# Moving all nine adaLN modulations of a two-layer trunk onto TensorE, 512 columns at a time in four column groups

## The chip, the cores and the metric

The kernel runs on one core of one Trainium2 chip. The metric is the device time of one execution in microseconds (us); lower is better. Three timed runs of the kernel before are shown, and one profiled execution.

## What is computed

The reference is one step of a diffusion trunk of two layers. 384 tokens of width 1024 pass through it: 128 context tokens and 256 latent tokens. Each layer is a SwiGLU, a token mixer of four parallel branches, and a second SwiGLU, all with residuals. Ahead of each of the three, the residual is normalised, scaled and shifted by vectors that depend on a conditioning vector; a third vector gates the result. These nine vectors of 1024 are the modulations of the layer:

```python
mod = jnp.einsum('bd,de->be', jax.nn.silu(cond), lp['w_ada']) + lp['b_ada']
mod = mod.reshape(cond.shape[0], N_MOD, 1, D_MODEL)
h = rms_norm(x, lp['norm_g'][0]) * (1.0 + mod[:, 1]) + mod[:, 0]
x = x + 0.5 * mod[:, 2] * swiglu(h, lp['ffn_w_gate'][0], lp['ffn_w_up'][0], lp['ffn_w_down'][0])
h = rms_norm(x, lp['norm_g'][1]) * (1.0 + mod[:, 4]) + mod[:, 3]
mix, state = token_mix(h, lp, l, cache)
x = x + mod[:, 5] * mix
h = rms_norm(x, lp['norm_g'][2]) * (1.0 + mod[:, 7]) + mod[:, 6]
x = x + 0.5 * mod[:, 8] * swiglu(h, lp['ffn_w_gate'][1], lp['ffn_w_up'][1], lp['ffn_w_down'][1])
```

There are two conditionings, one for the context tokens and one for the latent tokens, so each modulation is a product of two vectors of 1024 with a matrix of 1024 by 1024. `w_ada` has 9216 columns a layer. Modulations 0 and 1 of layer 0 are needed before the first SwiGLU can begin.

## The kernel before

The residual lies in the core's memory with its features on the 128 partitions and the 384 tokens as columns. Products of weights and residual are done in three matmuls, `mm3` (lines 184 to 188): weights and residual are each split into a rounded part and a rest, and hi by hi, hi by lo and lo by hi are added up. `split_unit` (lines 165 to 174) makes the two parts of a piece of weights: ScalarE casts to `whi` (line 169), VectorE or GpSimd subtracts to get `wlo` (line 173). There are three buffers of each.

A SwiGLU (`ffn_body`, lines 443 to 499) is a loop over 11 pieces of the hidden width, each with one load of gate weights and one of up weights of 1 MB and 96 matmuls (tiles `pg` and `pu`), and then a loop of the down product in two halves (tile `pd`), 528 matmuls. That is 1056 + 528 = 1584 matmuls of 384 columns for each of the four SwiGLUs. In this text FFN 0.0 and 0.1 are the two of layer 0, FFN 1.0 and 1.1 those of layer 1, and the mixers lie between the two of a layer.

The modulations are computed in quarters of 256 columns, in two ways:

- `ada` (lines 258 to 292) loads a quarter of 1024 by 256, 1 MB, as a tile `araw`. For the context conditioning VectorE multiplies and adds eight slices (lines 268 and 271). For the latent one ScalarE multiplies (lines 269 and 274) and GpSimd adds (line 275). VectorE transposes in blocks and reduces (lines 278 and 279), and at the end of a call four matmuls with a selection matrix put the sums on the partitions (line 285, tile `xa`).
- `ada_rows` (lines 238 to 256) does a quarter on TensorE: eight f32 matmuls with a stationary operand of two columns, one for each conditioning, and 256 moving columns (line 246, tile `arow`), a copy and two transposes.

`start` (lines 372 to 398) computes modulations 0 and 1 of layer 0: three quarters with `ada`, five with `ada_rows`, in the order of the string `ORDER`. All other quarters run beside the SwiGLUs. `hook(n)` takes n of them after each of the 11 pieces (line 469) and one after each part of the down loop (line 492), at a priority lowered by 100. FFN 0.0 has 28 quarters, FFN 0.1 has 20, FFN 1.0 has 16, and FFN 1.1 has none.

The order of the instructions on each engine is set when the kernel is built: a scheduler puts them in the order of a simulated timeline and of their priorities. All loads named here are issued by SP, in one queue, in that order, and a load that waits for its buffer holds up the loads behind it.

Of the kernel before, what the change touches and what calls it, by code (L numbers as in the profile page):

```python
# [17 lines left out]
D = 1024  # L18
# [16 lines left out]
K_ID, K_SEL, K_ONE = 0, 128, 640  # L35
# [8 lines left out]
ORDER = "nsrsrsrrr"  # L44
RING, NT1, NT2 = 256 * 310, 6, 4
# [4 lines left out]
def host_constants():  # L50
# [12 lines left out]
    for r in range(4):  # L63
        c[:, K_SEL + 128 * r:K_SEL + 128 * (r + 1)] = i[None, :] == (32 * r + i[:, None] % 32)
# [15 lines left out]
def pack_vectors(x):  # L80
    """The small vectors of both layers as columns of 128."""
# [14 lines left out]
def lockstep(*tasks):  # L96
    """Issue several tasks a stage of each at a time."""
    tasks = list(tasks)
    while tasks:
        tasks = [t for t in tasks if next(t, t) is not t]  # L100


class Ring:
    """Tiles at consecutive offsets of one window of memory, each over the oldest ones."""
# [13 lines left out]
class Trunk:  # L118
# [75 lines left out]
    def hidden(self, w, name="mm"):  # L194
        """A product with the normed residual; the first ones are scaled by 1 / rms and shifted behind the product."""
# [17 lines left out]
    def setup(self):  # L213
# [10 lines left out]
        nc.scalar.activation(out=self.cond, in_=vec[:, 0:16], func=AF.Silu)  # L224
        xrs = []
# [12 lines left out]
    def ada_rows(self, l, quarters):  # L238
        """Quarters of the nine modulations on the tensor engine, for both conditionings."""
        nc = self.nc  # L240
        cond = self.cond.rearrange("p (s k) -> p k s", s=2)
        for mod, j in quarters:
            raw = self.wcols(self.I["w_ada"][l], mod * D + 256 * j)
            ps = self.pm.tile([2, 256], F32, tag="mm", name="arow")
            for kk in range(KD):
                nc.tensor.matmul(ps, cond[:, kk], raw[:, kk], start=(kk == 0), stop=(kk == KD - 1))
            row = self.ring.tmp([2, 256], "mrow")
            nc.scalar.copy(row, ps)
            tp = self.mxps([128, 2, 2])
            for q in range(2):  # L250
                nc.tensor.transpose(tp[:, q], row[:, 128 * q:128 * q + 128], self.k(K_ID)[0:2, 0:2])
            c = slice(8 * mod + 2 * j, 8 * mod + 2 * j + 2)
            nc.vector.tensor_tensor(self.mods[l][:, :, c].rearrange("p s k -> p k s"), tp,
                                    self.prm[l][:, R_B:R_B + 72][:, c].unsqueeze(2).to_broadcast([128, 2, 2]),
                                    op=ALU.add)
            yield

    def ada(self, l, mod, n=4):
        """The same beside the tensor engine, n quarters from a modulation on, one at a time."""
        nc = self.nc  # L260
        ap = self.ap
        xa = ap.tile([128, 2, 8 * n], F32, tag="xa", name="xa", bufs=1)
        for j in range(n):
            raw = ap.tile([128, KD, 256], F32, tag="araw", name="araw", bufs=2)
            c0 = mod * D + 256 * j
            nc.sync.dma_start(raw, self.I["w_ada"][l, :, c0:c0 + 256].rearrange("(k p) n -> p k n", p=128))
            acc = [ap.tile([128, 256], F32, tag="acc", name="acc", bufs=6) for _ in range(2)]
            nc.vector.tensor_scalar_mul(acc[0], raw[:, 0], self.cond[:, 0:1])
            nc.scalar.mul(acc[1], raw[:, 0], self.cond[:, 8:9])
            for kk in range(1, KD):  # L270
                nc.vector.scalar_tensor_tensor(  # L271
                    acc[0], raw[:, kk], self.cond[:, kk:kk + 1], acc[0], op0=ALU.mult, op1=ALU.add)
                t = ap.tile([128, 256], F32, tag="acc", name="acct", bufs=6)
                nc.scalar.mul(t, raw[:, kk], self.cond[:, 8 + kk:9 + kk])  # L274
                self.last_add = nc.gpsimd.tensor_tensor(acc[1], acc[1], t, op=ALU.add)  # L275
            for s in range(2):
                tr = ap.tile([128, 256], F32, tag="acc", name="accr", bufs=6)
                nc.vector.transpose(tr, acc[s])  # L278
                nc.vector.tensor_reduce(
                    xa[:, s, 8 * j:8 * j + 8], tr.rearrange("p (a b) -> p a b", b=32), axis=AX, op=ALU.add  # L280
                )
            yield
        ps = self.mxps([128, 2, 2 * n])
        for r in range(4):
            nc.tensor.matmul(
                ps, self.k(K_SEL + 128 * r), xa.rearrange("p s (k r) -> p s k r", r=4)[:, :, :, r],
                start=(r == 0), stop=(r == 3),
            )
        c = slice(8 * mod, 8 * mod + 2 * n)
        nc.vector.tensor_tensor(self.mods[l][:, :, c], ps,  # L290
                                self.prm[l][:, R_B:R_B + 72][:, c].unsqueeze(1).to_broadcast([128, 2, 2 * n]), op=ALU.add)
        yield
# [79 lines left out]
    def start(self):  # L372
# [22 lines left out]
        with self.after(self.last_add):  # L395
            for k in range(KD):
                self.norm_scale(k)
# [1087 lines left out]
```

## Time and profile before

| | us |
|---|---|
| runs, median of 3 | 2246.99 |
| lowest, highest of the runs | 2241.5, 2248.05 |
| span of the profiled execution | 2244.0 |
| TensorE busy (matmuls) | 2076.3 |
| VectorE busy | 1724.6 |
| ScalarE busy | 1039.3 |
| GpSimd busy | 942.2 |

The span runs from the first to the last instruction of the profiled execution; that execution's own time as a run is not given apart, so sums are made against the span. Busy time is the union of an engine's instructions. Matmuls overlap in the records, so a mean duration is longer than the distance from one matmul to the next; where the price of a matmul is wanted, count the matmuls in a full stretch. An f32 matmul that is not in the rounded form stands as two instructions in the trace. Tile names are those of the program without buffer numbers.

### The profile page before, as it was taken

What the parts mean: (1) busy time and instruction counts of PE and PEld (TensorE: products, weight loads), DVE (VectorE), ACT (ScalarE), POOL (GpSimd) and SP (SyncE); (2) the same over time, 40 slices, a digit from 0 to 9 for tenths busy, and PEclk for the clock granted to TensorE, in tenths of its full rate; (3) what the DMA queues carried; (4) which work ended last, traced back from release to release, by engine and by line L of the source; (5) the groups of instructions that cost most, each with busy time, mean ns of one, the idle gap of its engine ahead of it and who ended that gap; (6) DMA issues with size and microseconds to landing.
All of it is one profiled execution on the core that took longest, in us unless ns stands there. A gap on an engine that the chain in (4) does not pass through costs nothing. (4 is left out here: it accounts for less than half of the span.)

```text
span 2244.0 us, 33102 instructions
## 1 busy us (share of the span) xinstructions
PE 2076.3 (93%) x12150; PEld 1992.7 (89%) x12150; DVE 1724.6 (77%) x3198; ACT 1039.3 (46%) x1978; POOL 942.2 (42%) x855
## 2 busy tenths in 40 slices
PE   6988888999789997998998999999987999999999
PEld 3988788999679997998887999998976899999999
DVE  8999998778995469999899974467999745764433
ACT  5666554634234235765556643354333332463322
POOL 5556666433655237366476520134354531500000
PEclk8999999999889999999999999999998999999999
DMA  9466655444333244566555644344442321444342
GB/s 306 152 217 199 202 198 164 129 136 105 83 81 103 60 164 155 169 210 214 186 193 155 206 135 133 128 146 137 119 95 83 109 76 59 160 134 129 115 139 76
DMA packets 316515, 323.08 MB, mean 144 GB/s; under 512 B 42112, under 2 KB 287296, under 8 KB 315840
## 3 DMA queue, kind: packets, MB, share of 16 engines
q1 hardware_dynamic: 316080, 320.70, 46.1%
q8 instruction: 95, 1.56, 0.3%
q14 instruction: 68, 0.56, 0.1%
q10 hardware_dynamic: 272, 0.26, 0.0%
HBM read 313.25 MB, written 7.69 MB: 143 GB/s over the span
## 5 line engine op out<-in xcount | busy, mean ns | idle before, releaser
L169 ACT CAST whi<-raw 128x1024 fp32r<-128x1024 f32 x422 | 440.2, 1045 | 511.1 <-PE mg L187 133.3
L173 DVE TENSOR_TENSOR wlo<-raw,whi 128x1024 fp32r<-128x1024 f32 x324 | 434.8, 1343 | 226.9 <-ACT whi L169 223.8
L275 POOL TENSOR_TENSOR acc<-acc,acct 128x256 f32<-128x256 f32 x469 | 440.5, 939 | 334.7 <-ACT acct L274 306.4
L173 POOL TENSOR_TENSOR wlo<-raw,whi 128x1024 fp32r<-128x1024 f32 x98 | 244.9, 2505 | 289.9 <-ACT whi L169 244.2
L271 DVE SCALAR_TENSOR_TENSOR acc<-araw,cond,acc 128x256 f32<-128x256 f32 x469 | 323.5, 690 | 6.3
L274 ACT ACTIVATE acct<-araw,cond 128x256 f32<-128x256 f32 x469 | 214.1, 501 | 139.7 <-DVE accr L278 83.4
L188 PE MATMUL pd<-hh,wlo 128*128 128x384 f32 x704 | 240.8, 345 | 20.2 <-DVE wlo L173 20.2
L186 PE MATMUL pd<-hh,whi 128*128 128x384 f32 x704 | 240.5, 342 | 9.0 <-ACT whi L169 4.5
L187 PE MATMUL pd<-hl,whi 128*128 128x384 f32 x704 | 239.9, 341 | 0.0
L188 PE MATMUL pg<-hhi,wlo 128*128 128x384 f32 x544 | 184.8, 340 | 19.2 <-DVE wlo L173 19.0
L188 PE MATMUL pu<-hhi,wlo 128*128 128x384 f32 x544 | 184.7, 340 | 13.4 <-DVE wlo L173 13.1
L186 PE MATMUL pg<-hhi,whi 128*128 128x384 f32 x544 | 182.1, 335 | 0.4 <-ACT whi L169 0.4
L187 PE MATMUL pu<-hlo,whi 128*128 128x384 f32 x544 | 182.2, 335 | 0.0
L186 PE MATMUL pu<-hhi,whi 128*128 128x384 f32 x544 | 182.2, 335 | 0.0
L187 PE MATMUL pg<-hlo,whi 128*128 128x384 f32 x544 | 182.1, 335 | 0.0
L186 PE MATMUL mg<-hhi,whi 128*128 128x384 f32 x512 | 177.7, 347 | 0.0
L187 PE MATMUL mg<-hlo,whi 128*128 128x384 f32 x512 | 175.4, 343 | 0.0
L188 PE MATMUL mg<-hhi,wlo 128*128 128x384 f32 x512 | 174.5, 343 | 0.5 <-DVE wlo L173 0.5
L321 POOL TENSOR_SCALAR xg<-xT,gs 128x128 f32<-128x128 f32 (+1 forms) x96 | 101.9, 1074 | 150.9 <-DVE xT L432 150.8
L188 PEld LDWEIGHTS pd<-hh,wlo 128*128 128x128 f32 x704 | 134.0, 191 | 27.6 <-DVE wlo L173 27.6
L186 PEld LDWEIGHTS pd<-hh,whi 128*128 128x128 f32 x704 | 134.4, 191 | 11.3 <-ACT whi L169 5.4
L187 PEld LDWEIGHTS pd<-hl,whi 128*128 128x128 f32 x704 | 134.5, 191 | 0.1
(410 smaller groups left out, 4961.5 us busy)
## 6 DMA issues: line engine op xcount, KB each, us to landing
araw<-in_w_ada SPq DMA_DIRECT2D x67, 1024.0 KB
raw<-in_w_in SPq DMA_DIRECT2D x62, 1024.0 KB
raw<-in_ffn_w_gate SPq DMA_DIRECT2D x44, 1024.0 KB
raw<-in_ffn_w_up SPq DMA_DIRECT2D x44, 1024.0 KB
raw<-in_ffn_w_down SPq DMA_DIRECT2D x40, 1024.0 KB
raw<-in_w_branch SPq DMA_DIRECT2D x16, 512.0 KB
raw<-in_w_out SPq DMA_DIRECT2D x8, 1024.0 KB
raw<-in_w_ada SPq DMA_DIRECT2D x5, 1024.0 KB
```

Source lines behind the costliest of these rows:

```text
L169: nc.scalar.copy(hi, src)
L173: (eng or nc.vector).tensor_tensor(lo, src, hi.bitcast(F32), op=ALU.subtract)
L186: nc.tensor.matmul(ps, w[0], x[0], start=start, stop=False)
L187: nc.tensor.matmul(ps, w[0], x[1], start=False, stop=False)
L188: nc.tensor.matmul(ps, w[1], x[0], start=False, stop=stop)
L271: nc.vector.scalar_tensor_tensor(acc[0], raw[:, kk], self.cond[:, kk:kk + 1], acc[0], op0=ALU.mult, op1=ALU.add)
L274: nc.scalar.mul(t, raw[:, kk], self.cond[:, 8 + kk:9 + kk])
L275: self.last_add = nc.gpsimd.tensor_tensor(acc[1], acc[1], t, op=ALU.add)
L321: self.nc.gpsimd.tensor_scalar(xg[kk][:, a:e], self.xT[:, kk, a:e], gs[:, s, kk:kk + 1], None, op0=ALU.mult)
```

## The change

`ada_rows` and the old `ada` go. A new `ada` computes halves of 512 columns on TensorE. The 1024 rows of a half come in two loads of 1 MB, each a tile `araw` of four slices of 128 rows. The stationary operand, `cond32`, is the two conditionings padded with zeros to 32 columns. Slice g of a load goes to column group g, the partitions 32g to 32g + 31 of the result. So a half is eight f32 matmuls, and each column group holds the sum over two slices. One copy, four transposes of 128 columns and a reduction over the four groups finish it.

```diff
+        self.cond32 = self.const.tile([128, KD, 32], F32, name="cond32")
+        nc.vector.memset(self.cond32, 0.0)
+        nc.vector.tensor_copy(self.cond32[:, :, 0:2], self.cond.rearrange("p (s k) -> p k s", s=2))
...
+    def ada(self, l, *halves):
+        nc = self.nc
+        for mod, hf in halves:
+            c0 = mod * D + 512 * hf
+            ps = self.mxps([128, 512], "arow")
+            for i in range(2):
+                raw = self.ap.tile([128, 4, 512], F32, tag="araw", name="araw", bufs=self.n_araw)
+                self.last_load = nc.sync.dma_start(raw, self.I["w_ada"][l, 512 * i:512 * i + 512, c0:c0 + 512].rearrange(
+                    "(k p) n -> p k n", p=128))
+                for g in range(4):
+                    nc.tensor.matmul(ps[32 * g:32 * g + 32], self.cond32[:, 4 * i + g], raw[:, g],
+                                     start=(i == 0), stop=(i == 1), tile_position=(0, 32 * g))
+            row = self.ring.tmp([128, 512], "mrow")
             nc.scalar.copy(row, ps)
+            tp = self.mxps([128, 4, 128], "acol")
+            for q in range(4):
+                nc.tensor.transpose(tp[:, q], row[:, 128 * q:128 * q + 128], self.k(K_ID))
+            t = self.small.tile([128, 2, 4], F32, tag="asum", name="asum")
+            nc.vector.tensor_reduce(t, tp.rearrange("p q (g e) -> p e q g", g=4)[:, 0:2], axis=AX, op=ALU.add)
+            c = slice(8 * mod + 4 * hf, 8 * mod + 4 * hf + 4)
+            nc.vector.tensor_tensor(self.mods[l][:, :, c], t,
+                                    self.prm[l][:, R_B:R_B + 72][:, c].unsqueeze(1).to_broadcast([128, 2, 4]), op=ALU.add)
             yield
...
+        for j, _ in enumerate(self.ada(0, (1, 0), (1, 1))):
+            if j == 0:
                 self.rstd()
...
+        for _ in self.ada(0, (0, 0), (0, 1)):
+            pass
         self.early_shift()
...
-            hook(2)
+            hook(1)
         if nxt is None:
             self.nx = None
         else:
             self.norm_begin(*nxt)
-            self.scales(*nxt, self.nx[2])
...
                 hook(1)
+            if nxt is not None and dg == 0:
+                self.scales(*nxt, self.nx[2])
...
+            self.n_araw = 4
             with self.pool("ap") as self.ap:
                 self.start()
+            self.n_araw = 3
...
-                self.ffn(l, 0, self.ada(l, 5, 16) if l else chain(self.ada(l, 2, 12), self.ada(l, 5, 16)), (l, 1))
+                mods = {(0, 0): ((0, 2, 8),), (0, 1): ((0, 8, 9), (1, 0, 3)), (1, 0): ((1, 3, 8),), (1, 1): ((1, 8, 9),)}
+                jobs = [chain(*(self.ada(m, *((k, hf) for k in range(a, e) for hf in range(2)))
+                                for m, a, e in mods[l, i])) for i in range(2)]
+                self.ffn(l, 0, jobs[0], (l, 1))
...
-                self.ffn(l, 1, iter(()) if l else self.ada(1, 0, 20), None if l else (1, 0))
+                self.ffn(l, 1, jobs[1], None if l else (1, 0))
```

The halves are spread over all four SwiGLUs now: 12 in FFN 0.0, 8 in FFN 0.1, 10 in FFN 1.0 and 2 in FFN 1.1, one hook after each piece; four are in the start. The three buffers of `araw` beside the SwiGLUs (four in the start) hold a half and a half. The selection matrices leave the table of constants, and `RING`, the size of the window of temporary memory, goes from 256 * 310 to 256 * 309.

The change moves instructions at three places that matter here. In names such as `pu_1019` the number is a buffer's.

On TensorE, modulation work reached a SwiGLU before only as the four matmuls on `xa` at the end of a call, here in the down product of FFN 0.0:

```order
L186 MATMUL pd_3490<-hh_2805,whi_3807 128x384
L187 MATMUL pd_3490<-hl_2806,whi_3807 128x384
L285 MATMUL mx_3649<-xa_1992,cst_82 128x64 x4
L188 MATMUL pd_3490<-hh_2805,wlo_3808 128x384
L186 MATMUL pd_3491<-hh_2526,whi_3801 128x384
```

Now every half puts eight `arow` matmuls among those of an up product, here in FFN 0.0; the piece shows where the half goes over from its first load to its second:

```order
L185 MATMUL pu_1019<-hhi_339,wlo_991 128x384
L252 MATMUL arow_894<-araw_895,cond32_91 32x512
L183 MATMUL pu_1019<-hhi_339,whi_990 128x384
L184 MATMUL pu_1019<-hlo_340,whi_990 128x384
L252 MATMUL arow_894<-araw_901,cond32_91 32x512
```

The `arow` matmuls stand one by one between matmuls of the up product, and not four together.

On VectorE, a piece of the SwiGLU's gate and up loop was full of products and reductions for the modulations before:

```order
L271 SCALAR_TENSOR_TENSOR acc_946<-araw_944,cond_89,acc_946 128x256
L278 STREAM_TRANSPOSE accr_978<-acc_946 128x256
L278 STREAM_TRANSPOSE accr_981<-acc_947 128x256
L268 TENSOR_SCALAR acc_1132<-araw_1130,cond_89 128x256
L279 TENSOR_REDUCE xa_665<-accr_978 128x8
L464 TENSOR_TENSOR sg_1123<-sg_1123,pu_1098 128x384
L279 TENSOR_REDUCE xa_665<-accr_981 128x8
L271 SCALAR_TENSOR_TENSOR acc_1132<-araw_1130,cond_89,acc_1132 128x256
L173 TENSOR_TENSOR wlo_1280<-raw_1210,whi_1279 128x1024
```

In the same loop now:

```order
L427 TENSOR_TENSOR sg_1044<-sg_1044,pu_1019 128x384
L170 TENSOR_TENSOR wlo_1144<-raw_1074,whi_1143 128x1024
L431 TENSOR_TENSOR hl_1048<-sg_1044,hh_1047 128x384
L170 TENSOR_TENSOR wlo_1148<-raw_1076,whi_1147 128x1024
L260 TENSOR_REDUCE asum_914<-acol_909 128x8
L262 TENSOR_TENSOR mods0_87<-asum_914,vec_83 128x2x4
L427 TENSOR_TENSOR sg_1136<-sg_1136,pu_1111 128x384
```

A half leaves one reduction and one addition on VectorE, between the splits of the weights.

On TensorE at the start, just ahead of the first SwiGLU, quarters of two kinds ended the chain before:

```order
L246 MATMUL arow_386<-raw_384,cond_89 2x256 x8
L246 MATMUL arow_413<-raw_411,cond_89 2x256 x8
L251 MATMUL mx_397<-cst_82,mrow_395 128x2 x2
L251 MATMUL mx_424<-cst_82,mrow_422 128x2 x2
L285 MATMUL mx_428<-xa_182,cst_82 128x12 x4
L186 MATMUL pg_519<-xs_160,whi_511 128x386
```

Now the last two of the four halves do:

```order
L252 MATMUL arow_267<-araw_268,cond32_91 32x512 x4
L252 MATMUL arow_267<-araw_274,cond32_91 32x512 x4
L258 MATMUL acol_282<-cst_82,mrow_280 128x128 x4
L252 MATMUL arow_290<-araw_291,cond32_91 32x512 x4
L252 MATMUL arow_290<-araw_297,cond32_91 32x512 x4
L258 MATMUL acol_305<-cst_82,mrow_303 128x128 x4
L183 MATMUL pg_398<-xs_163,whi_390 128x386
```

Here the four column groups of a load stand together.

## Rows read from the trace of the kernel before

**Rows 1.** The page, busy time (share of the span) and instructions of each engine.
```profile
PE 2076.3 (93%) x12150; PEld 1992.7 (89%) x12150; DVE 1724.6 (77%) x3198; ACT 1039.3 (46%) x1978; POOL 942.2 (42%) x855
```

**Rows 2.** Windows of the start and the four SwiGLUs; columns in the first line.
```profile
core 0: us, PE busy (x) PEld busy (x) DVE busy (x) ACT busy (x) POOL busy (x), PEclk, DMA share, GB/s
0.00:48.60 48.60, 29.24 (x132) 14.20 (x132) 39.62 (x91) 25.91 (x61) 24.57 (x33) 0.88 0.93 300
48.60:382.60 334.00, 297.86 (x1601) 283.12 (x1602) 322.03 (x531) 200.13 (x385) 211.34 (x224) 0.97 0.60 192
...
864.80:1192.40 327.60, 292.31 (x1603) 281.48 (x1602) 310.33 (x508) 194.02 (x373) 192.46 (x201) 0.98 0.59 190
1192.40:1484.50 292.10, 283.25 (x1604) 279.67 (x1603) 195.10 (x314) 137.68 (x235) 80.63 (x86) 0.99 0.47 146
...
1958.20:2239.00 280.80, 280.06 (x1614) 279.35 (x1613) 126.46 (x183) 103.50 (x155) 7.90 (x6) 1.00 0.36 116
```

**Rows 3.** Timeline of TensorE: start us, us, engine, line, operation; two edges.
```profile
48.60 0.69 PE L186 MATMUL pg<-xs,whi 128*128 128x386 f32 x1 [3.34 <-ACT xs L332]
...
2238.67 0.34 PE L188 MATMUL pd<-hh,wlo 128*128 128x384 f32 x1
```

**Rows 4.** Waits of TensorE in FFN 0.0: us in total, times, longest.
```profile
PE pg L188 <- DVE wlo L173: 11.6, 13, 2.1
PE pd L188 <- DVE wlo L173: 11.5, 11, 2.1
```

**Rows 5.** Groups by line and shape: busy us, mean ns of one | idle before.
```profile
L275 POOL TENSOR_TENSOR acc<-acc,acct 128x256 f32<-128x256 f32 x469 | 440.5, 939 | 334.7 <-ACT acct L274 306.4
...
L271 DVE SCALAR_TENSOR_TENSOR acc<-araw,cond,acc 128x256 f32<-128x256 f32 x469 | 323.5, 690 | 6.3
...
L274 ACT ACTIVATE acct<-araw,cond 128x256 f32<-128x256 f32 x469 | 214.1, 501 | 139.7 <-DVE accr L278 83.4 <-POOL acc L275 42.2 <-DVE xa L279 13.3
...
L279 DVE TENSOR_REDUCE xa<-accr 128x8 f32<-128x256 f32 x134 | 50.7, 406 | 0.1
```

**Rows 6.** Windows again, a stretch inside the up product of FFN 1.1.
```profile
2016.00:2072.00 56.00, 56.00 (x325) 56.00 (x324) 24.21 (x28) 19.56 (x28) 0.00 (x0) 1.00 0.45 145
```

**Rows 7.** Timeline of TensorE in the start, and durations (min/median/max ns) of `arow`.
```profile
23.24 7.07 PE L246 MATMUL arow<-raw,cond 128*2 128x256 f32 x32
...
L246 PE MATMUL arow<-raw,cond x80: 378/379/635, 15.9 to 42.1; 128*2 128x256 f32 x80
```

**Rows 8.** Timeline of TensorE around a lone score matmul of the attention.
```profile
611.32 0.33 PE L187 MATMUL mg<-hlo,whi 128*128 128x384 f32 x1
611.49 0.34 PE L188 MATMUL mg<-hhi,wlo 128*128 128x384 f32 x1
611.76 0.91 PE L1057 MATMUL mx<-bkTs,bqT 32*128 32x384 f32 x2
612.60 0.45 PE L186 MATMUL mg<-hhi,whi 128*128 128x384 f32 x1
612.88 0.34 PE L187 MATMUL mg<-hlo,whi 128*128 128x384 f32 x1
```

**Rows 9.** Durations (min/median/max ns) of the score matmuls.
```profile
L1057 PE MATMUL mx<-bkTs,bqT x64: 481/585/1005, 607.9 to 1770.5; 32*128 32x384 f32 x64
```

**Rows 10.** Timeline of TensorE: three transposes of 128 columns at the end.
```profile
2238.85 0.49 PE L1430 MATMUL mx<-cst,xT 128*128 128x128 f32 x3
...
L1430 PE MATMUL mx<-cst,xT x24: 269/272/331, 2190.5 to 2240.0; 128*128 128x128 f32 x24
```

**Rows 11.** Windows again, a stretch of the start in which loads flow.
```profile
4.00:22.00 18.00, 10.14 (x40) 5.61 (x40) 13.31 (x21) 7.39 (x17) 5.95 (x7) 0.81 1.07 352
```

**Rows 12.** Timeline of TensorE: three score matmuls in a row.
```profile
607.91 0.92 PE L1057 MATMUL mx<-bkTs,bqT 32*128 32x384 f32 x6 [0.37 <-DVE bkTs L1044]
```

**Rows 13.** Windows again, a stretch of the mixers of layer 0.
```profile
560.00:616.00 56.00, 44.35 (x226) 38.42 (x223) 54.55 (x116) 13.11 (x21) 35.34 (x26) 0.88 0.32 85
```

More of the change, by code (lines that the diff above doesn't have):

```diff
@@ L33 @@
 C_MERGE = 3872
-K_ID, K_SEL, K_ONE = 0, 128, 640
+K_ID, K_ONE = 0, 128
 NC1 = K_ONE + 2
@@ L43 @@
 EARLY = (10, 7)
-ORDER = "nsrsrsrrr"
-RING, NT1, NT2 = 256 * 310, 6, 4
+RING, NT1, NT2 = 256 * 309, 6, 4
 R_G, R_B, R_CV, R_NG, R_RT, R_N = 0, 24, 96, 114, 118, 122
@@ L62, in host_constants @@
     c[:, K_PB:K_PB + 128] = 128 - i[None, :]
-    for r in range(4):
-        c[:, K_SEL + 128 * r:K_SEL + 128 * (r + 1)] = i[None, :] == (32 * r + i[:, None] % 32)
     c[:, K_KP] = 127 - i
@@ L235, in setup @@
                 nc.vector.tensor_copy(self.xT[:, 4 * hf:4 * hf + 4, 128 * b:128 * b + 128], tp)
-    def ada_rows(self, l, quarters):
+    def ada(self, l, *halves):
         nc = self.nc
[L241 to L247, printed above, removed]
-            nc.scalar.copy(row, ps)
[L249 to L255, printed above, removed]
-            yield
@@ L258, in ada @@
[L258 to L292, printed above, removed]
@@ L377, in start @@
         self.early_open()
-        shift, rows = self.ada(0, 0, ORDER.count("s")), self.ada_rows(
-            0, [(1, j) for j in range(4)] + [(0, j) for j in range(ORDER.count("s"), 4)])
-        j = 0
-        for c in ORDER:
-            if c == "n":
-                self.rstd()
-            elif c == "s":
-                next(shift)
-            else:
-                next(rows)
-                if j < 4:
-                    self.scales(0, 0, self.nx[2], 2 * j, 2 * j + 2)
-                    self.early_part(2 * j, True)
-                    self.early_part(2 * j + 1, True)
-                j += 1
-        next(shift)
+        for j, _ in enumerate(self.ada(0, (1, 0), (1, 1))):
+            if j == 0:
+                self.rstd()
+            self.scales(0, 0, self.nx[2], 4 * j, 4 * j + 4)
+            for k in range(4 * j, 4 * j + 4):
+                self.early_part(k, True)
+        for _ in self.ada(0, (0, 0), (0, 1)):
+            pass
         self.early_shift()
-        with self.after(self.last_add):
-            for k in range(KD):
-                self.norm_scale(k)
+        for k in range(KD):
+            self.norm_scale(k)
         self.norm()
```

## The prediction, before the changed kernel ran

> **What bounds the kernel now.** I read the engine totals first [rows 1]: TensorE is busy for 93% of the span, VectorE for 77%, GpSimd for 42%. An average over unlike stages does not say which engine sets the end, so the second view is the table of windows by stage [rows 2]. Its first row is the start, its other four are the SwiGLU stages in the order they run: both of layer 0, both of layer 1. All four hold the same 1584 wide matmuls; the rest of their TensorE counts is small change. They take 334.0, 327.6, 292.1 and 280.8 us, and their edges are the first `pg` and the last `pd` matmul on TensorE's timeline; the first and the last of these eight stand in [rows 3]. The last stage has no modulation work at all: TensorE is busy for 280.06 of 280.80 us, and VectorE for 126.46. In the first two, VectorE is busy for 322.03 of 334.0 and for 310.33 of 327.6 us, while TensorE loses time. So the two stages with most modulation work are bound by VectorE, the last one by TensorE. The waits of the first stage say the same from the other side: TensorE waits for `wlo` [rows 4]. What the modulations cost today is therefore 334.0 + 327.6 + 292.1 + 280.8 - 4 x 280.8 = **111.3 us**, although their own instructions are busy for far longer [rows 5]: 323.5 us of products on VectorE, 440.5 us of sums on GpSimd, 214.1 us of products on ScalarE. Most of that lies beside TensorE's work.
>
> The price of plain TensorE work comes from a quiet window of the last stage [rows 6]: 325 matmuls of 384 columns in 56.00 us, 0.172 us each.
>
> **What the change removes.** All of [rows 5] goes. If the new work were free, each SwiGLU stage would fall to the 280.8 us of the last one: **-111.3 us**. VectorE, ScalarE and GpSimd get back hundreds of microseconds, but once TensorE bounds a stage nothing waits for them. What they still do for a half modulation (a copy on ScalarE, a short reduction like the 406 ns one in [rows 5] and an add on VectorE) hides: VectorE has over 150 us free in a stage like the last of [rows 2].
>
> **What it adds on TensorE.** 36 halves of 8 matmuls (32 by 512, f32) and 4 transposes. Four halves are in the start, 32 in the SwiGLU stages (12, 8, 10 and 2). The price of a column: two instructions make one f32 matmul (40 matmuls of the old `arow` stand as x80), and 32 of them follow each other in 7.07 us, the last of which is 0.38 long [rows 7]: (7.07 - 0.38)/31 = 0.216 us for 256 columns. So 512 columns cost 0.432 us an instruction and **0.863 us a matmul**, five plain matmuls' time.
>
> Whether four column groups share that time depends on the order. In the start they stand four in a row. In the SwiGLU stages they do not: a full-width `pu` or `pd` matmul stands between almost any two of them. Of the 256, 222 stand alone; the other 34 are in seven pieces (one of 8, four of 5, two of 3). A matmul on a part of the array that stands alone between full ones has a row here: the attention's score matmul, 32 rows of the array, 384 columns, two instructions [rows 8]. The full matmul ahead of it starts at 611.49, the second full one behind it at 612.88: 1.39 us, of which two plain steps are 0.34. It costs 1.05 us, and its columns stream for 2 x 384 x 0.843 ns = 0.65 us. The other **0.40 us** is going in and out: the part matmul starts 0.27 us after the full one instead of 0.17, the next full one 0.84 us after that for 0.65 of columns, and the second full one 0.28 us later instead of 0.17. Of a part matmul's two records the first is 0.10 us longer than the second (585 against 481 ns, [rows 9]), its weights. The pattern is the same wherever such a matmul stands alone.
>
> I take the same 0.40 for a column group, less 0.08 because the weights are 32 columns and not 128 (three quarters of those 0.10): 0.863 + 0.32 = **1.18 us** alone. Bounds: 0.863 with no going in and out, 1.26 with all of it; 1.18 is nearest to the row. So:
> - 222 alone x 1.18 = 262 us;
> - seven pieces, 12 rounds side by side x 0.863 + 7 x 0.32 = 12.6 us;
> - 32 x 4 transposes at (0.49 - 0.27)/2 = 0.11 us [rows 10] = 14 us.
>
> Sum **+288.6 us**, all on TensorE, which is full in these stages, so all of it on the path: 4 x 280.8 + 288.6 = 1412 us for the four.
>
> **The start** costs nothing either way, within 3 us. Before its first `pg` the old kernel moved 300 GB/s x 48.6 us = 14.6 MB [rows 2]; the new one must move 13.3 MB (eight 1.05 MB pieces of `w_ada`, three of FFN weights, the input and the tables), but its last two pieces feed a chain of passes, copy, transposes, reduction and shift of some 5 us, against the old chain's `next(shift)`. Loads here run at 352 GB/s at best [rows 11], so 13.3 MB take 38 to 44 us, and the chain ends at 43 to 49 us where it ended at 48.6.
>
> **The queue.** In the SwiGLU stages SP holds two `araw` pieces ahead of the next `up` and `gate` loads, and they wait for TensorE to finish the half before. That half is done more than one iteration before the loads behind are wanted. An iteration lasts 96 x 0.172 + 8 x 1.18 + 0.44 = 26.4 us and moves 4.2 MB, which 352 GB/s carry in 12. It costs nothing, under a cover of 14 us. The mixers keep their work: nothing, within 8 us for a moved order.
>
> **Sum.** 2244.0 - 111.3 + 288.6 = 2421.3 us against the profiled span. The median of the runs, 2247.0, lies 3.0 above that span, so **2424 us**.
>
> **The rivals.** *No going in and out* (0.15): a column group costs its stream alone, since its rows are the whole 128 and only the columns are part. Then 222 x 0.863 + 12 x 0.863 + 14 = 216 us, and 2247.0 - 111.3 + 216 = 2352. For it: the old `arow`, two columns wide without a place given, ran without gaps [rows 7]. Against it: those stood among their like, and [rows 8] is the only part of the array between full ones.
>
> *Column groups side by side although full matmuls stand between* (0.06), the way to faster. The score matmuls show that parts of the array run together when they are adjacent: three of them, six instructions, take 0.92 us [rows 12], as long as the one alone. If TensorE also kept four column groups together across the `pu` rows, a half would cost 2 x 0.863 + 0.40 + 0.44 = 2.6 us and 32 of them 82: 2247.0 - 111.3 + 82 = 2218, faster. It decides at (111.3 - 14)/256 = 0.38 us a matmul. Against it: in [rows 8] the full matmuls wait for the part to end. The Trainium skill's page "TensorE: Matmul & The Clock Gate", section on packing small matmuls, speaks against my sum: it says that outputs placed at different column groups run concurrently, three of them 2.38 times as fast; by it the sum would be this rival's. [rows 12] agree for adjacent ones; no row shows it across a full matmul.
>
> *A lower clock* (0.07). The granted clock is 0.88 of full speed in a window of the attention where TensorE is idle for 12 of 56 us [rows 13], so some of it ran at 1.2 and not 2.4 GHz. If the gaps around column groups did as much to all four stages, it would cost 1412/0.88 - 1412 = 193 us: 2617. Against it: nothing lets TensorE idle long, and 32 old `arow` passes in a row kept their pace [rows 7].
>
> That the change does not do what it says is part of the forecast: four column groups at a time happens in the start alone.
>
> **How the numbers follow.** The forecast has 0.72: slower by 177 us, 7.9%. The range takes in no going in and out (2352, less 7 for the mixers and the start) below, and above the full 0.40 (+18) with as much again for a dearer way in and out and the order of the mixers: **2345 to 2475**. It leaves out the side-by-side and the clock cases, 0.13. What a measurement can tell from no change is 0.3%, 7 us. Faster by more than that is the side-by-side rival alone, 0.06; within it 0.01, a column-group matmul of 0.35 to 0.41 us; slower 0.93.
>
> **What would show it.** In the profile after, the four stages should last about 395, 353, 372 and 293 us with TensorE near 100% and VectorE under half; where full matmul and lone `arow` alternate, the pair should repeat every 1.35 us (1.18 + 0.17); the start should show its passes in groups of four a few ns apart. If VectorE still ends the waits for `wlo` in the SwiGLU stages, if `arow` matmuls wait for their loads, or if the pairs repeat every 1.05 us or less, the prediction is wrong in that step.

## The result, and the profile after

The changed kernel takes **2407.19 us** (median of 4 runs, 2404.26 to 2410.82) against 2247.52 us for the kernel before: 1.072 times as long, with an interval of 1.070 to 1.074. The forecast was 2424 us, range 2345 to 2475, slower. The profiled span went from 2244.0 to 2402.6 us.

The page of the changed kernel, busy time of each engine, to set beside [rows 1]:

```profile
PE 2320.9 (97%) x12740; PEld 2027.0 (84%) x12740; DVE 1265.3 (53%) x2454; ACT 836.8 (35%) x1473; POOL 491.3 (20%) x386
```

VectorE lost 459 us of busy time, GpSimd 451, ScalarE 203. TensorE gained 245, and the time rose. The windows by stage of the changed kernel, to set beside [rows 2]:

```profile
core 0: us, PE busy (x) PEld busy (x) DVE busy (x) ACT busy (x) POOL busy (x), PEclk, DMA share, GB/s
0.00:44.50 44.50, 22.98 (x114) 10.22 (x114) 26.61 (x69) 20.03 (x44) 13.86 (x20) 0.71 1.01 352
44.50:437.20 392.70, 392.70 (x1825) 296.44 (x1826) 126.95 (x203) 110.64 (x165) 13.87 (x19) 0.99 0.45 149
437.20:912.40 475.20, 447.63 (x2801) 429.62 (x2800) 357.30 (x779) 186.89 (x380) 209.42 (x152) 0.96 0.38 115
912.40:1261.50 349.10, 349.10 (x1755) 289.16 (x1754) 133.57 (x212) 113.01 (x173) 17.56 (x18) 1.00 0.45 148
1261.50:1631.10 369.60, 369.60 (x1796) 292.47 (x1796) 136.00 (x227) 115.18 (x179) 21.18 (x25) 1.00 0.44 143
1631.10:2106.90 475.80, 447.35 (x2801) 428.33 (x2800) 358.01 (x779) 186.84 (x380) 209.60 (x152) 0.96 0.39 115
2106.90:2397.30 290.40, 290.40 (x1654) 280.34 (x1654) 125.75 (x186) 103.49 (x155) 5.82 (x4) 1.00 0.35 115
```

In all four SwiGLU stages TensorE is busy for the whole window: it is the only bound, and VectorE is under half. The stages add up to 1401.8 us where they were 1234.5, +167.3, more than the whole +158.6 us; the start gives back 4.1 and the mixers 4.9. The waits for `wlo` [rows 4] are gone; the only wait of TensorE that the list gives for FFN 0.0 is this one:

```profile
PE pg L183 <- ACT xs L304: 0.7, 1, 0.7
```

TensorE's timeline in the up product of FFN 0.0 (start us, us, operation) shows where the time went:

```profile
138.22 1.05 PE L252 MATMUL arow<-araw,cond 128*32 128x512 f32 x2
139.20 0.45 PE L185 MATMUL pu<-hhi,wlo 128*128 128x384 f32 x1
139.57 1.04 PE L252 MATMUL arow<-araw,cond 128*32 128x512 f32 x2
140.55 0.44 PE L183 MATMUL pu<-hhi,whi 128*128 128x384 f32 x1
140.92 1.05 PE L252 MATMUL arow<-araw,cond 128*32 128x512 f32 x2
```

From one `arow` to the next it is 1.35 us, of which the full matmul between them is worth 0.17. Each `arow` stands alone here, as 222 of the 256 beside the SwiGLUs do, so the four column groups don't meet. In the start they do: the x8 below are four matmuls of two instructions, all four together in 1.06 us, about as long as one alone above. They wait for the load of `araw`.

```profile
11.20 1.06 PE L252 MATMUL arow<-araw,cond 128*32 128x512 f32 x8 [1.12 <-DMA araw<-in_w_ada]
13.81 1.06 PE L252 MATMUL arow<-araw,cond 128*32 128x512 f32 x8 [1.55 <-DMA araw<-in_w_ada]
```

### The profile page after: what moved, and what is told of

Read it like the earlier page. It is cut to its first block, busy times and chain, and to the rows that moved or that the text cites. A ratio compares the mean times of both kernels' runs of the same rounds, so it can differ in the third digit from the quotient of the medians.

```text
span 2402.6 us, 32115 instructions
## 1 busy us (share of the span) xinstructions
PE 2320.9 (97%) x12740; PEld 2027.0 (84%) x12740; DVE 1265.3 (53%) x2454; ACT 836.8 (35%) x1473; POOL 491.3 (20%) x386
## 5 line engine op out<-in xcount | busy, mean ns | idle before, releaser
L170 DVE TENSOR_TENSOR wlo<-raw,whi 128x1024 fp32r<-128x1024 f32 x324 | 401.0, 1238 | 453.3 <-ACT whi L166 444.6
L293 POOL TENSOR_SCALAR xg<-xT,gs 128x128 f32<-128x128 f32 (+1 forms) x96 | 89.5, 946 | 1059.7 <-DVE xT L395 1038.0
L252 PE MATMUL arow<-araw,cond 128*32 128x512 f32 x576 | 256.7, 640 | 6.4 <-DMA araw<-in_w_ada 6.4
L185 PE MATMUL pd<-hh,wlo 128*128 128x384 f32 x704 | 235.6, 338 | 0.0
L427 DVE TENSOR_TENSOR sg<-sg,pu 128x384 f32<-128x384 f32 x68 | 37.7, 554 | 338.7 <-PE pu L185 338.7
L183 PE MATMUL pu<-hhi,whi 128*128 128x384 f32 x544 | 190.3, 350 | 0.0
L184 PE MATMUL pu<-hlo,whi 128*128 128x384 f32 x544 | 189.4, 348 | 0.0
L183 PEld LDWEIGHTS pu<-hhi,whi 128*128 128x128 f32 x544 | 102.0, 187 | 62.0 <-issue 62.0
L185 PEld LDWEIGHTS pu<-hhi,wlo 128*128 128x128 f32 x544 | 102.1, 188 | 60.4 <-issue 60.4
L184 PEld LDWEIGHTS pu<-hlo,whi 128*128 128x128 f32 x544 | 102.1, 188 | 43.6 <-issue 43.6
```

What stands on the lines that cost most here:

```text
L170: (eng or nc.vector).tensor_tensor(lo, src, hi.bitcast(F32), op=ALU.subtract)
L183: nc.tensor.matmul(ps, w[0], x[0], start=start, stop=False)
L184: nc.tensor.matmul(ps, w[0], x[1], start=False, stop=False)
L185: nc.tensor.matmul(ps, w[1], x[0], start=False, stop=stop)
L252: nc.tensor.matmul(ps[32 * g:32 * g + 32], self.cond32[:, 4 * i + g], raw[:, g], start=(i == 0), stop=(i == 1), tile_position=(0, 32 * g))
L293: self.nc.gpsimd.tensor_scalar(xg[kk][:, a:e], self.xT[:, kk, a:e], gs[:, s, kk:kk + 1], None, op0=ALU.mult)
```

## The experiments

The first question was the price on TensorE: is it the missing neighbours, or the f32 matmuls themselves? The second, which the first answers raised, was what the old way had really cost. Where one run is given, it has no interval; the runs of the kernel before lie between 2240.1 and 2251.0 us, so a difference of a few us between two single runs says little.

### Neighbours: the eight matmuls of a half together

Nothing else is changed than the order. `self.after(x)` puts an instruction behind `x` in the order of its engine; `last_mm` is the last matmul of the `mm3` before, `last_arow` the last modulation matmul:

```diff
-        nc.tensor.matmul(ps, w[0], x[0], start=start, stop=False)
+        with self.after(self.last_arow if start else None):
+            nc.tensor.matmul(ps, w[0], x[0], start=start, stop=False)
...
+        self.last_mm = nc.tensor.matmul(ps, w[1], x[0], start=False, stop=stop)
...
+                    with self.after(self.last_mm if i + g == 0 else None):
+                        self.last_arow = nc.tensor.matmul(
```

> Two ordering edges are added for each half of a modulation, so that its eight modulation matmuls stand next to each other on TensorE's queue beside the SwiGLU too, where nearly all of them stood alone between full matmuls. Theory (each lone matmul pays its whole 0.86 us and 0.32 us for going in and out of a column group; neighbours in four column groups run side by side, as they do at the start): a half then takes two passes and one going in and out, about 2.05 + 0.44 = 2.5 us; 32 halves x 2.5 = 80 us on top of four SwiGLU stages at 278.6 us, 1194 us where the changed kernel has 1402, so about 2199 us, faster than the kernel before. Rival (beside full matmuls the four groups are not shared even where they are neighbours): eight passes of 0.86 us and one going in and out, about 7.2 us a half, and the time about 2363 us, slower than before.

Measured: **2202.49 us** (4 runs), ratio to the kernel before 0.9805, interval 0.9788 to 0.9822. The same instructions in another order turn 7% slower into 2% faster. Its timeline of TensorE:

```profile
159.27 1.92 PE L255 MATMUL arow<-araw,cond 128*32 128x512 f32 x16
161.13 0.44 PE L185 MATMUL pg<-hhi,whi 128*128 128x384 f32 x1
161.41 0.34 PE L186 MATMUL pg<-hlo,whi 128*128 128x384 f32 x1
```

Eight matmuls (x16) are through in 1.86 us, where eight lone ones take 8 x 1.18 = 9.4. The Trainium skill's page "TensorE: Matmul & The Clock Gate", section on packing small matmuls, gives 2.38 times for three column tiles; here four groups of neighbours take 1.86 us for 8 x 0.863 = 6.9 us of columns, 3.7 times. So the gain is there where the matmuls are neighbours, and the changed kernel shows none where they aren't.

### No column groups: one group for all, or the whole array

```diff
-                    nc.tensor.matmul(ps[32 * g:32 * g + 32], self.cond32[:, 4 * i + g], raw[:, g],
-                                     start=(i == 0), stop=(i == 1), tile_position=(0, 32 * g))
...
+                    nc.tensor.matmul(ps[0:32], self.cond32[:, 4 * i + g], raw[:, g],
+                                     start=(i + g == 0), stop=(i == 1 and g == 3), tile_position=(0, 0))
```

> All eight modulation matmuls of a half go through the first column group, one after the other, and add into the same 32 PSUM partitions; the sum over groups on VectorE goes. The order on TensorE stays much as in the changed kernel. Theory (the column groups of lone matmuls were never shared, so losing them costs only the few that had neighbours): the seven or so grouped halves become about 17 us longer and the start about 10 us, about 2430 us in all (2420 to 2445). Rival (groups overlap also across the full matmuls between them, so that the lone ones did share something): losing the four groups costs on the lone ones too, over 2460 us.

Measured: 2432.4 us (one run). Taking three of the four column groups away costs 25 us, as expected: the lone matmuls shared nothing. Its pairs keep their 1.35 us:

```profile
138.54 1.04 PE L252 MATMUL arow<-araw,cond 128*32 128x512 f32 x2
139.52 0.44 PE L184 MATMUL pu<-hlo,whi 128*128 128x384 f32 x1
139.89 1.04 PE L252 MATMUL arow<-araw,cond 128*32 128x512 f32 x2
```

Then the stationary operand padded to all 128 columns, with no column group at all:

```diff
-        self.cond32 = self.const.tile([128, KD, 32], F32, name="cond32")
+        self.cond32 = self.const.tile([128, KD, 128], F32, name="cond32")
...
+                    nc.tensor.matmul(ps, self.cond32[:, 4 * i + g], raw[:, g],
+                                     start=(i + g == 0), stop=(i == 1 and g == 3))
```

> The modulation matmuls use the whole array: the stationary operand is 128 columns wide (the two conditionings and zeros), all eight of a half add into the same PSUM partitions, and the sum over groups on VectorE goes. The order on TensorE stays as in the changed kernel. Theory (the 0.32 us beyond the 0.86 us of a lone modulation matmul is the price of changing to a column group and back): it goes, 222 x 0.32 = 71 us in the SwiGLU stages; the start pays about 10 us for eight full passes a half in place of two shared ones; about 2345 us in all (2335 to 2362). Rival (the 0.32 us belongs to any float32 matmul that comes between float32r ones, whatever its width): no gain in the SwiGLU stages and the start longer, about 2415 us.

Measured: 2352.98 us (one run), within the theory's range, and the pair goes to 1.03 us:

```profile
138.41 1.02 PE L252 MATMUL arow<-araw,cond 128*128 128x512 f32 x2
138.87 0.74 PE L183 MATMUL pu<-hhi,whi 128*128 128x384 f32 x1
139.44 1.02 PE L252 MATMUL arow<-araw,cond 128*128 128x512 f32 x2
```

1.35 - 1.03 = 0.32 us: going into a column group and out, measured by itself. A lone matmul is cheaper here on four times as much of the array.

The weight loads (PEld) show where most of it goes; first the changed kernel, then the whole array (start us, us, idle before):

```profile
139.57 0.14 PEld L252 LDWEIGHTS arow<-araw,cond 128*32 128x32 f32 x2 [0.19 <-issue]
140.54 0.19 PEld L183 LDWEIGHTS pu<-hhi,whi 128*128 128x128 f32 x1 [0.84 <-issue]
```

```profile
138.84 0.19 PEld L183 LDWEIGHTS pu<-hhi,whi 128*128 128x128 f32 x1 [0.24 <-issue]
139.27 0.36 PEld L252 LDWEIGHTS arow<-araw,cond 128*128 128x128 f32 x2 [0.24 <-issue]
```

With the column group, `arow`'s first weights (0.11 us) start to load at 139.57 with their matmul, and the weights of the full matmul behind (0.19 us) at 140.54, 0.84 us after the load before, with theirs. With the whole array, `arow`'s weights start at 139.27, 0.17 us ahead of their matmul at 139.44, and the full matmul's 0.24 us after the load before. Two loads that no longer run beside matmuls, 0.11 + 0.19 us, come near the 0.32; no run tests this apart.

### Twice in and out for each half

The edges were set for groups of four, one load at a time (`last_mm` ahead of the first of each load, `last_arow` ahead of every `mm3`).

> As the grouped kernel, but the edges keep four modulation matmuls together (those of one load) in place of eight, so TensorE goes into the column groups and out of them twice a half. Theory (a half costs two shared passes and 0.44 us for each going in and out): 32 x 0.44 = 14 us over the grouped kernel's 2202 us, about 2216 us (2208 to 2222). Rival (the price is not paid for each change of the way in which the array is divided): no difference from 2202 us.

Measured: 2198.31 us (one run), no dearer at all. That was a miss of the edit, not of the price: in the trace the two fours of a half stand together in all 32 halves beside the SwiGLUs, and one half that the first grouped kernel had left alone is grouped as well. The next run sets them apart:

```diff
             for i in range(2):
+                if i and self.n_araw == 3:
+                    yield
```

> As the kernel with edges for groups of four, in which the two groups of a half came to stand together all the same; now the second four of a half are issued one step of the program later, so that full matmuls come between. Theory (a half costs two shared passes, and 0.44 us for each time TensorE goes into the column groups and out): 32 x 0.44 = 14 us over that kernel's 2198 us, about 2212 us (2206 to 2218). Rival (going in and out costs little between groups, and only lone matmuls pay it): 2200 us or less.

Measured: 2212.88 us (one run), 14.6 us more. In the trace 61 of the 64 groups of four stand alone now and three are split into three and one, so TensorE goes in and out 67 times where it did 32 times. Around one of the 61:

```profile
99.87 0.34 PE L187 MATMUL pu<-hhi,wlo 128*128 128x384 f32 x1
100.14 1.06 PE L257 MATMUL arow<-araw,cond 128*32 128x512 f32 x8
101.13 0.45 PE L185 MATMUL pg<-hhi,whi 128*128 128x384 f32 x1
101.42 0.34 PE L186 MATMUL pg<-hlo,whi 128*128 128x384 f32 x1
```

From the full matmul ahead to the second one behind it is 1.55 us, of which two plain steps are 0.35 and the columns 0.86: 0.34 for the way in and out of a group, about that of a lone matmul. The theory's time came out, but not by its price: 0.44 was too much, and what adds up to about the 14.6 is 35 more ways at 0.34 (12 us) and three more passes (2.6 us).

### The floor: no modulation work beside the SwiGLUs

```diff
-                    nc.tensor.matmul(ps[32 * g:32 * g + 32], self.cond32[:, 4 * i + g], raw[:, g],
...
+                    if self.n_araw == 4:
+                        nc.tensor.matmul(ps[32 * g:32 * g + 32], self.cond32[:, 4 * i + g], raw[:, g],
...
+                    elif g == 0:
+                        nc.vector.tensor_copy(t[:, i], raw[:, 0, 0:4])
```

> Leaves out the modulation matmuls, their transposes and sums beside the SwiGLUs (all modulations but the first two of layer 0 are filled with a slice of the weights); the weights are still loaded. It measures the floor under all ways of doing that work. Theory (with it gone, each SwiGLU stage is as long as its own matmuls, 278.6 us, since neither the loads nor anything else waits there): four stages 1114 us, about 2119 us in all. Rival (some of what the changed kernel gained in these stages against the kernel before is lost to loads or to buffers, whatever does the modulations): stages of 285 us and more, 2145 us or above.

Measured: 2124.09 us (one run), near the theory. Its four SwiGLU windows:

```profile
44.10:323.50 279.40, 279.40 (x1587) 279.40 (x1588) 127.99 (x216) 104.57 (x153) 14.08 (x20) 0.99 0.62 209
803.20:1082.00 278.80, 278.36 (x1595) 277.66 (x1595) 138.61 (x242) 108.60 (x166) 18.31 (x18) 1.00 0.68 236
1081.80:1360.10 278.30, 278.30 (x1598) 278.26 (x1597) 135.82 (x205) 109.47 (x169) 20.84 (x25) 1.00 0.39 126
1838.70:2117.50 278.80, 278.80 (x1615) 278.32 (x1613) 124.03 (x182) 102.68 (x153) 4.71 (x4) 1.00 0.35 117
```

They add up to 1115.3 us. So the old way had cost 1234.5 - 1115.3 = 119.2 us, the new way costs 1401.8 - 1115.3 = 286.5, and a grouped half (2198.31 - 2124.09)/32 = 2.32 us, its transposes included.

### What the old way had cost, engine by engine

These two runs each leave out one of the two chains of the kernel before:

```diff
-            nc.vector.tensor_scalar_mul(acc[0], raw[:, 0], self.cond[:, 0:1])
...
-                nc.vector.scalar_tensor_tensor(
-                    acc[0], raw[:, kk], self.cond[:, kk:kk + 1], acc[0], op0=ALU.mult, op1=ALU.add)
```

> The kernel before without VectorE's chain of products for the first conditioning (it leaves that part of the modulations out; the other conditioning's sums are transposed in its place); ScalarE's products, GpSimd's sums and all loads stay. Theory (VectorE alone bound the first two SwiGLU stages of the kernel before): the stages fall to about 280 us each, 115 us in all, and the time to about 2130 us (2122 to 2150). Rival (the chain through ScalarE and GpSimd, or the loads, held these stages as well): 2200 us or more.

Measured: 2143.78 us (one run), within the theory's range. But the other half of the test:

```diff
-            nc.scalar.mul(acc[1], raw[:, 0], self.cond[:, 8:9])
...
-                nc.scalar.mul(t, raw[:, kk], self.cond[:, 8 + kk:9 + kk])
-                self.last_add = nc.gpsimd.tensor_tensor(acc[1], acc[1], t, op=ALU.add)
```

> The kernel before without ScalarE's products and GpSimd's sums for the second conditioning (it leaves that part of the modulations out; the other conditioning's sums are transposed in its place); VectorE's products and all loads stay. Theory (VectorE alone bound the first two SwiGLU stages): VectorE has the same work, the stages stay about as long, and the time about 2235 us (2215 to 2250). Rival (the chain through ScalarE and GpSimd held these stages as much as VectorE): 2190 us or less.

Measured: 2131.64 us (one run). The theory fell: with all its own products left, VectorE still let the stages fall. So the next run took GpSimd's sums alone away (the last line of the diff), with ScalarE's products in place.

> The kernel before without GpSimd's sums for the second conditioning (it leaves them out, so that conditioning's modulations lack most of their terms); ScalarE's products, VectorE's products and all loads stay. It asks why leaving out ScalarE's and GpSimd's part gave as much as leaving out VectorE's. Theory (GpSimd's sums stretch VectorE's instructions that read two tiles: a product took 696 ns with them and 483 ns without them and ScalarE's products): VectorE's products take some 480 ns and its splits some 1220 ns, and the time is about 2133 us (2125 to 2145). Rival (ScalarE's products and their traffic stretch them): 690 ns and 1470 ns as in the kernel before, and over 2200 us.

Measured: 2141.21 us (one run), the theory's time: with ScalarE's products in place, leaving out GpSimd's sums is enough. In these three runs the four stages take 1134 to 1136 us, some 20 over the floor, so neither chain is free by itself. The groups of VectorE between 48 and 320 us (busy us, mean ns of one | idle before), first in the kernel before:

```profile
L271 DVE SCALAR_TENSOR_TENSOR acc<-araw,cond,acc 128x256 f32<-128x256 f32 x167 | 116.2, 696 | 2.3
L173 DVE TENSOR_TENSOR wlo<-raw,whi 128x1024 fp32r<-128x1024 f32 x54 | 79.4, 1473 | 0.0
L278 DVE STREAM_TRANSPOSE accr<-acc 128x256 f32<-128x256 f32 x46 | 17.8, 421 | 1.8 <-DVE acc L271 0.5
L468 DVE TENSOR_TENSOR hl<-sg,hh 128x384 fp32r<-128x384 f32 x22 | 17.6, 802 | 0.0
L464 DVE TENSOR_TENSOR sg<-sg,pu 128x384 f32<-128x384 f32 x17 | 9.2, 540 | 0.0
```

and in the kernel without GpSimd's sums:

```profile
L271 DVE SCALAR_TENSOR_TENSOR acc<-araw,cond,acc 128x256 f32<-128x256 f32 x196 | 94.7, 483 | 2.9
L173 DVE TENSOR_TENSOR wlo<-raw,whi 128x1024 fp32r<-128x1024 f32 x64 | 78.2, 1221 | 9.1 <-ACT whi L169 7.2 <-DMA raw<-in_w_in 1.4
L277 DVE STREAM_TRANSPOSE accr<-acc 128x256 f32<-128x256 f32 x56 | 21.6, 423 | 0.5
L467 DVE TENSOR_TENSOR hl<-sg,hh 128x384 fp32r<-128x384 f32 x22 | 12.2, 553 | 0.0
L463 DVE TENSOR_TENSOR sg<-sg,pu 128x384 f32<-128x384 f32 x17 | 9.4, 553 | 6.0 <-PE pu L188 5.3
```

FFN 0.0 in that kernel, to set beside [rows 2], and `hl` in the one without VectorE's chain:

```profile
43.40:324.20 280.80, 280.58 (x1602) 280.07 (x1603) 255.63 (x531) 195.36 (x385) 19.01 (x24) 0.99 0.72 229
```

```profile
L465 DVE TENSOR_TENSOR hl<-sg,hh 128x384 fp32r<-128x384 f32 x22 | 22.4, 1017 | 1.2 <-ACT hh L464 1.2
```

Read the means in pairs. The product goes from 696 to 483 ns, the split `wlo` from 1473 to 1221, `hl` from 802 to 553: these three read two tiles from the core's memory (SBUF). The transpose, with one input, and `sg`, whose second input `pu` lies in PSUM, stay; the first product of each chain, which reads one tile, changes little (341 to 322 ns). The Trainium skill's page "SBUF — State Buffer", section "Who interferes with whom", says that a VectorE instruction with two SBUF inputs contends with a GpSimd instruction that reads SBUF, and that one with at most one SBUF input, outside the modes that use both ports, doesn't. The trace agrees, with 44 and 45% more on the product and on `hl` and 21% on `wlo`. In FFN 0.0 that is 196 x 0.213 + 66 x 0.252 + 22 x 0.249 = 64 us of VectorE, about what its busy time falls by there (322.03 to 255.63 us).

### Some of the old work beside grouped matmuls

Three kernels compute everything and give part of the 32 halves back to the other engines, in the old way or in one without GpSimd. In the first, every second half goes the old way (in the second, two of three, `n % 3`):

```diff
+    jobs.append(chain(*(self.ada_old(m, k, hf) if (n % 2) else self.ada(m, (k, hf))
+                        for n, (m, k, hf) in enumerate(hs))))
```

> On top of the edges for groups of four, every second half modulation beside the SwiGLUs is computed in the way of the kernel before, on VectorE, ScalarE and GpSimd, and only the other 16 halves go through TensorE. A grouped half was measured at (2198 - 2124) / 32 = 2.32 us over the kernel without modulations beside the SwiGLUs. Theory (VectorE loses TensorE time only when it fills a stage; in the first SwiGLU stage it would be busy for 127 us of its own and 12 quarters x 7 us, some 211 of 294 us): 2124 + 16 x 2.32 + some 5 us for the four small matmuls of each half, about 2166 us, faster than both kernels. Rival (any modulation work on VectorE makes the split of the weights late, as in the third stage of the kernel before, which lost some 13 us with VectorE busy for two thirds): some 10 us more in three stages, about 2196 us, no gain over the kernel with all halves grouped.

> As the kernel with every second half on VectorE, ScalarE and GpSimd, but two of three halves go that way and 11 of 32 through TensorE. Theory (VectorE would be busy for about 127 + 16 x 7 = 239 of 290 us in the first stage, still under its limit): 2124 + 11 x 2.32 + 7 us, about 2157 us, some 9 us under the kernel with every second half. Rival (from about there on VectorE's queue makes the split of the weights late): 2166 us or more, no better than every second half.

Measured: 2203.73 us for every second half (ratio 0.9819, 0.9800 to 0.9838) and 2206.98 us for two of three (0.9828, 0.9811 to 0.9846): on the rivals' side, no gain over grouping alone. The first one's waits of TensorE between 48 and 320 us, and its window of FFN 0.0:

```profile
PE pu L189 <- DVE wlo L173: 3.2, 3, 1.4
PE pd L189 <- DVE wlo L173: 1.0, 1, 1.0
```

```profile
44.50:350.80 306.30, 302.11 (x1753) 289.78 (x1754) 212.64 (x341) 146.43 (x255) 94.41 (x103) 0.99 0.60 192
```

VectorE is at 69% of FFN 0.0, and TensorE still loses 4.2 us to the split. The other part is TensorE's own: it is busy for 302.1 us here, since the selector matmuls of a half take about 1 us (48 instructions, 6.2 us busy, for the six halves of FFN 0.0) and not the 0.3 that I had put. So a half moved saves 1.3 us instead of 2. The 16 save 18 us of TensorE's busy time in the four stages, but it idles 15 us more there (11.7 behind the split), and the mixers take 9 us more. With two of three halves moved TensorE idles 17 us in the stages, and the split is only 3.5 of them; 4.7 are behind ScalarE's cast `whi`. Both kernels have a shorter ring of tiles as well (256 * 298 for 256 * 309); whether it has a part wasn't tried.

Last, every second whole modulation on VectorE alone, both conditionings, with neither ScalarE nor GpSimd:

```diff
+            for s in range(2):
...
+                nc.vector.tensor_scalar_mul(acc, raw[:, 0], self.cond[:, 8 * s:8 * s + 1])
+                for kk in range(1, KD):
+                    nc.vector.scalar_tensor_tensor(
+                        acc, raw[:, kk], self.cond[:, 8 * s + kk:8 * s + kk + 1], acc, op0=ALU.mult, op1=ALU.add)
```

> On top of the kernel with all halves grouped (2198 us): every second whole modulation beside the SwiGLUs, 7 of 16, is computed on VectorE alone, for both conditionings, without ScalarE and GpSimd; the other 18 halves go through TensorE in groups. Theory (with GpSimd idle VectorE's instructions keep their short times; 12 quarters x 9.1 us = 109 us beside its own 127 us in the first stage of some 290 us; the four small selector matmuls of a modulation cost about 1 us, as measured for those of a half): 2198 - 14 x 2.32 + 7 x 1.0 = about 2172 us (2163 to 2190), faster than every kernel so far that computes all. Rival (work on VectorE beside the SwiGLUs makes TensorE wait whatever its form, as in the two mixed kernels): 2196 us or more.

Measured: **2185.4 us** (4 runs), ratio 0.9738, interval 0.9709 to 0.9768, within the theory's range but 13 us above its 2172: the fastest of all that compute everything. VectorE's product stays short although it does both conditionings. Its group between 48 and 320 us, and the windows of FFN 0.0 and of the mixers of layer 0:

```profile
L286 DVE SCALAR_TENSOR_TENSOR acc<-araw,cond,acc 128x256 f32<-128x256 f32 x137 | 66.4, 484 | 2.7
```

```profile
44.80:340.60 295.80, 295.78 (x1722) 285.75 (x1723) 210.65 (x410) 107.84 (x158) 12.32 (x19) 0.99 0.62 197
340.60:831.80 491.20, 450.63 (x2808) 430.42 (x2807) 372.50 (x804) 188.33 (x381) 208.80 (x153) 0.96 0.37 112
```

VectorE does as much as in the kernel with every second half, 211 us in FFN 0.0, and TensorE doesn't wait. That fits GpSimd as what made the splits late; the two kernels differ in more, so this pair alone doesn't show it. The four stages fall from 1192.7 us (all halves grouped) to 1163.0, more than the 25.5 expected. The mixers give back 16.6 of it: those of layer 0 take 491.2 us for 480.0, with 804 VectorE instructions for 779, and 14 of VectorE's products for modulations stand there, up to 359 us: some of that work runs over into them. Whether the shorter ring of tiles in this kernel (256 * 301) has a part in it wasn't tried.

## Why the prediction was right

The sum against the span was 2421.3 us and came out at 2402.6, 18.7 lower. All its terms erred to the same side, so no error hid another.

- **The price of a lone column-group matmul, 1.18 us**, was right: the pairs repeat every 1.35 us as forecast, and its two parts were measured apart: 0.863 of columns and, with the whole array in its place, 0.32 less. The attention's score matmul [rows 8] was a good row to price it by. The 0.08 taken off for narrower weights fits the loads: 0.11 us for 32 columns, 0.18 for the score matmul's 128.
- **+288.6 us on TensorE** measured 286.5 over the floor.
- **-111.3 us for the old work** was mis-sized: it measured -119.2. The step that failed is taking the 280.8 us of FFN 1.1 as the floor of all four; without modulations they last 278.3 to 279.4, and FFN 1.1 itself 278.8. Four times some 2 us is most of the error in the stages (10 us). FFN 1.1 had no modulations to lose; half of what it gained is one wait (shown below).
- **The cause given for that term** was half right. "Bound by VectorE" holds, but VectorE was full because GpSimd's sums stretched its two-input instructions. Either chain taken away brings the four stages within some 20 us of the floor. The size didn't suffer, since the change removes both.
- **The stages**, forecast at 395, 353, 372 and 293 us, are 392.7, 349.1, 369.6 and 290.4. **The start**, 0 within 3 us, gained 4.1; its chain ended within the 43 to 49 us given. It ran with a granted clock of 0.71, which did cost something (shown below). **The mixers**, 0 within 8, gained 4.9 in sum.
- **The rivals.** Side by side across full matmuls fell with the one-group kernel: nothing had been shared. No going in and out fell with the pairs. A lower clock: the stages ran at 0.99 and 1.00. One argument against it was weak, though: the 32 `arow` passes of [rows 7] kept their pace, but the other 32 in a row of the same start took 8.59 us for those 7.07, with a granted clock of 0.82 from 33.9 to 42.5 us:

```profile
33.94 8.59 PE L246 MATMUL arow<-raw,cond 128*2 128x256 f32 x32
```

The wait at the head of FFN 1.1, in the kernel before:

```profile
PE pg L187 <- DVE xs L341: 0.7, 1, 0.7
```

With the step behind it, it cost about 1.0 us; the kernel without modulations has no such wait there. The other 1.2 us are spread over many steps, and why isn't settled.

The last eight modulation matmuls of the start, in the changed kernel:

```profile
37.77 3.66 PE L252 MATMUL arow<-araw,cond 128*32 128x512 f32 x16
```

They waited for no load, and eight of them take 1.92 us in the grouped kernel beside the SwiGLUs, where the clock is full. So by estimate the start could have gained up to some 2 us more.

What the prediction didn't see is how near the other sign was. 2218 us stood there as the price if the groups shared, and two ordering edges for each half gave 2202.

## What to carry to other kernels

In this kernel parts of the array ran together only where their matmuls were neighbours in the order that the scheduler left: read that order, and tie a group together with edges, before counting on it. A lone matmul of 32 columns was cheaper here padded to the whole array. An idle engine isn't free help: price a GpSimd operation with what it does to VectorE's two-input instructions beside it. And a full engine may be full of stretched instructions, so look at the mean duration of one with its neighbour idle before saying what binds it.

## What was unexpected of the hardware

- GpSimd's sums made VectorE's two-input instructions 21 to 45% longer (1221 to 1473, 553 to 802, 483 to 696 ns); with VectorE's chain of products gone and GpSimd's sums left, `hl` even took 1017 ns on average, and why isn't known.
- A matmul of 32 columns between full ones took 0.32 us longer than one of 128 columns at the same place.
- Eight matmuls in four column groups take 1.86 us as neighbours and 9.4 us apart (8 x 1.18), with the same instructions.
